# Query normalisation moved behind the rotary products in a two-layer attention and recurrence step

## Chip, cores and metric

The kernel runs on one core of one Trainium2 chip. The metric is device time in microseconds (us); lower is better. TensorE multiplies matrices into PSUM, VectorE (DVE in the profile), ScalarE (ACT) and GpSimd (POOL) do elementwise work, and SyncE (SP) issues most weight transfers. Each engine executes its own queue of instructions in order and waits at semaphores.

## The reference

The reference is one inference step of a two-layer diffusion trunk over 512 latent tokens and 128 context tokens, in float32, with a model width of 1024. Layer 0 is gated attention with 16 query heads and 4 key/value heads of 64; layer 1 is a bidirectional gated linear recurrence. What matters here is how the queries of layer 0 are made:

```python
def _rms_norm(x, g):
    y = xf * lax.rsqrt(jnp.mean(xf * xf, axis=-1, keepdims=True) + NORM_EPS)
    return (y * g.astype(jnp.float32)).astype(x.dtype)

def _attn_project(h, w_in, q_gain, k_gain):
    proj = h @ w_in
    q, k, v, g = jnp.split(proj, ...)
    q = _rms_norm(q.reshape(B, L, N_HEADS, HEAD_DIM), q_gain)
    ...

def _apply_rope(x, cos, sin):      # latent tokens only
    rotated = jnp.concatenate([rot_half(xr), rot_half(xc)], axis=-1)
    return (xf * cos + rotated * sin).astype(x.dtype)
```

Each head of each token is divided by its root mean square, multiplied by a gain, and, for latent tokens, rotated. The factor 1/rms is one number for each token and head, and the rotation is linear in the head's 64 values, so that the factor may stand on either side of the rotation.

## The kernel before

All matrix products of the projections are done as three float32r products of high and low parts (`whi` and `wlo` for weights, `hhi` and `hlo` for activations). Tokens are handled in three units, `UNITS = ((0, 2), (2, 2), (4, 1))`: two pairs of 128-token latent tiles, and one tile of 128 context tokens, called the prompt unit here. The query heads come in four chunks of four heads (256 columns). Chunk 0 is made in `lead_in`, at the start, by functions of its own use (`rms_apply` and `rope_apply` on `q0`), which the change leaves as they are. Chunks 1 to 3 are made by the generator `q_gen`, which runs as a side job of the attention: `weave(att, side, SIDE_B)` advances the side job by 0.62 of a step for each step of the attention, and a `yield` ends a step. Chunk c + 1 may start when the attention's front has reached chunk c.

For each unit `q_gen` does the following. `tok_unit` multiplies 24 or 48 times into one PSUM bank named `qmm`, out of a ring of three banks that the attention's transposes (`pt`), the query transposes (`qps`) and the adaptive projection (`adaps`) share. `rms_stat` squares it on ScalarE (`sq`, L510), sums on VectorE (`ss`, L511), and takes the power -1/2 on GpSimd (`rstd`, L187). After a yield the previous unit's split query is transposed by TensorE (`qps`, L582) and copied to `X` (L584); then a piece of the adaptive projection is made (`fill`, with the loads of its weights), and two more yields follow. Then `rms_apply` multiplies PSUM by `rstd` into `qn` (L524, pinned to the program order), and `rope_apply` makes `u = qn * sin` (L537), `r = qn * cos` (L539) and adds the exchanged halves (L541); for the prompt unit it makes `r = qn * gain` alone (L533). The gain of the latent tokens is folded into the tables `cosq` and `sinq`. After another yield `q_split` writes the high part of `r` with ScalarE (`qs`, L574) and the low part with VectorE (`qs`, L575). The next chunk's `Weights` are split by `split_piece`: `whi` on ScalarE (L221), `wlo` on VectorE (L222), from 512 KB pieces `raw` that the SP queue loads (L208) into a ring of three buffers. The same ring takes the pieces of the adaptive projection, `in_ada_s`.

The attention itself works on score tiles `sc` (L731, L732), takes the negative maximum `nm` on VectorE (L825), the exponential `p` on ScalarE (L828), its scaling by GpSimd (L833), transposes `pt` (L840), and the product with the values `pot` (L758).

The order in which each engine gets its instructions is not simply that of the program: the whole first layer stands in one block, `tc.block(schedule_with_timeline_sim=True)`, whose planner orders instructions by modelled times. An instruction in `tc.keep_in_program_order(...)` is pinned against others so marked.

## Time and profile before

| | |
|---|---|
| median of 3 runs | 873.47 us (872.31 to 873.93) |
| profiled execution, its own time | 873.58 us |
| span of the profiled execution | 871.8 us |
| mean granted TensorE clock | 0.986 |
| TensorE busy | 819.8 us (94%) |
| VectorE busy | 533.8 us (61%) |
| ScalarE busy | 373.0 us (43%) |
| GpSimd busy | 212.9 us (24%) |

The span is the time from the first to the last instruction of the profiled execution. In the tables below an instruction is named by engine, line, operation and tiles, written as output<-input; times are in us from the start of the span. In the views of waits the columns are the total waiting time in us, how often, and the longest. In the views of stretches the columns are the stretch, its length, the busy us and instruction counts of TensorE's matmuls, its weight loads, VectorE, ScalarE and GpSimd, then the granted TensorE clock, the share of DMA engines busy and GB/s. A busy time of TensorE at a granted clock of 0.50 is work that takes about half of that at full clock.

### The profile page before, as it was taken

The numbers are of one execution on the slowest core, as the hardware profiler recorded it, in microseconds if no ns is written. First come the engines' busy times: TensorE is split into PE (matmuls) and PEld (weight loads), VectorE is DVE, ScalarE is ACT, GpSimd is POOL, SyncE is SP. The second block draws the span as 40 slices with busy tenths as digits, with TensorE's granted clock in tenths as the row PEclk, the third lists the DMA queues.
The fourth block names the chain that finished last, engine by engine and source line by source line (L and its number), as shares of the span: only waits on it lengthen the run. The fifth ranks groups of instructions, "written<-read, shape, count | busy, mean of one in ns | idle before, by whom it ended". The sixth has DMA issues, their size and how long they took to land.

```text
span 871.8 us, 19257 instructions
## 1 busy us (share of the span) xinstructions
PE 819.8 (94%) x8120; PEld 732.0 (84%) x8120; DVE 533.8 (61%) x952; ACT 373.0 (43%) x735; POOL 212.9 (24%) x263
## 2 busy tenths in 40 slices
PE   6999999979899988999999999999999999979794
PEld 4789998858778766888899999999999999977683
DVE  3656435735746666676437575758577576757485
ACT  2232536544655767222434444345354443453100
POOL 0213002533424644110001314042333243211010
PEclk9999999989999999999999999999999999989998
DMA  9932212162232253631223323332323232241131
GB/s 339 356 98 85 79 44 74 50 211 87 73 128 67 79 172 120 217 121 40 94 71 72 104 60 88 77 105 68 110 59 114 67 94 84 81 182 50 55 121 48
DMA packets 33991, 92.50 MB, mean 106 GB/s; under 512 B 5025, under 2 KB 12209, under 8 KB 33905
## 3 DMA queue, kind: packets, MB, share of 16 engines
q1 hardware_dynamic: 22416, 71.90, 24.5%
q0 software_dynamic: 4864, 14.44, 5.5%
q10 hardware_dynamic: 6624, 4.93, 1.9%
q8 instruction: 64, 1.05, 0.5%
q14 instruction: 23, 0.18, 0.1%
HBM read 82.06 MB, written 9.19 MB: 105 GB/s over the span
## 4 chain that ended last, share of the span: by engine, by line
PE 85%; DVE 5%; DMA 3%; ACT 3%; issue 1%; POOL 1%; SPq 0%; DVEq 0%; ACTq 0%; POOLq 0%
PE rps L1116 7%; PE rps L1117 6%; PE rps L1118 6%; PE vgps L1106 5%; PE vgps L1108 4%; PE vgps L1107 4%; PE outp L1001 4%; PE outp L1002 4%; PE outp L1003 4%; PE pot L758 3%; PE pt L840 3%; PE lv L1246 2%; PE gps L327 2%; PE gps L328 2%; PE gps L329 2%; PE sc L731 2%
## 5 line engine op out<-in xcount | busy, mean ns | idle before, releaser
L1116 PE MATMUL rps<-h1hi,rhi 128*128 128x320 f32 x368 | 117.9, 320 | 0.0
L1117 PE MATMUL rps<-h1lo,rhi 128*128 128x320 f32 x368 | 113.7, 309 | 0.0
L1118 PE MATMUL rps<-h1hi,rlo 128*128 128x320 f32 x368 | 113.5, 309 | 0.0
L833 POOL TENSOR_SCALAR p<-p,rc 128x640 f32<-128x640 f32 x64 | 54.6, 858 | 70.7 <-DVE rc L832 61.3
L1116 PEld LDWEIGHTS rps<-h1hi,rhi 128*128 128x128 f32 x368 | 69.1, 188 | 1.3
L1117 PEld LDWEIGHTS rps<-h1lo,rhi 128*128 128x128 f32 x368 | 69.2, 188 | 0.0
L1118 PEld LDWEIGHTS rps<-h1hi,rlo 128*128 128x128 f32 x368 | 69.1, 188 | 0.0
L222 DVE TENSOR_TENSOR rlo<-raw,rhi 128x1024 fp32r<-128x1024 f32 x32 | 45.0, 1410 | 33.9 <-ACT rhi L221 33.9
L1274 POOL COPY At<-near 32x160 f32<-32x160 f32 x32 | 14.0, 438 | 201.3 <-DVE near L1236 200.3
L828 ACT ACTIVATE p<-sc,nm 128x640 f32<-128x640 f32 x64 | 51.0, 798 | 24.8 <-DVE nm L825 21.0
L825 DVE TENSOR_REDUCE nm<-sc 128x1 f32<-128x640 f32 x64 | 51.8, 818 | 15.5 <-PE sc L732 15.2
L1224 ACT COPY kc<-A 128x640 f32<-128x640 f32 x40 | 32.2, 804 | 57.7 <-DVE A L1255 51.1
L221 ACT CAST rhi<-raw 128x1024 fp32r<-128x1024 f32 x32 | 33.6, 1049 | 49.9 <-PE rps L1117 47.0
L1106 PE MATMUL vgps<-rhi,h1hi 128*128 128x256 f32 x180 | 51.5, 286 | 1.2 <-ACT h1hi L956 1.2
L840 PE MATMUL pt<-small,p 128*128 128x128 f32 x320 | 50.2, 280 | 2.2 <-DVE acc L316 1.4
L1108 PE MATMUL vgps<-rhi,h1lo 128*128 128x256 f32 x180 | 50.8, 282 | 0.4 <-DVE h1lo L957 0.4
L1107 PE MATMUL vgps<-rlo,h1hi 128*128 128x256 f32 x180 | 50.6, 281 | 0.0
L736 ACT COPY pts<-pt 128x512 f32<-128x512 f32 x64 | 36.2, 589 | 32.9 <-PE pt L840 32.5
L731 PE MATMUL sc<-kk,X 128*128 128x320 f32 x128 | 42.5, 341 | 4.7 <-ACT p L828 4.2
L840 PEld LDWEIGHTS pt<-small,p 128*128 128x128 f32 x320 | 37.1, 142 | 11.2 <-issue 6.2
L1106 PE MATMUL vgps<-wspare,h1hi 128*128 128x256 f32 x140 | 41.6, 297 | 0.0
L327 PE MATMUL gps<-hhi,whi 128*128 128x320 f32 x128 | 40.0, 312 | 0.4 <-ACT X L584 0.4
(265 smaller groups left out, 2373.2 us busy)
## 6 DMA issues: line engine op xcount, KB each, us to landing
raw<-in_rec_w_in SPq DMA_DIRECT2D x40, 512.0 KB, 3.8
raw<-in_ada_s SPq DMA_DIRECT2D x32, 512.0 KB, 3.8
raw<-in_ada_m SPq DMA_DIRECT2D x16, 512.0 KB, 7.7
raw<-in_attn_w_in SPq DMA_DIRECT2D x16, 512.0 KB, 4.3
raw<-in_attn_w_out SPq DMA_DIRECT2D x8, 512.0 KB, 4.2
raw<-in_rec_w_out SPq DMA_DIRECT2D x8, 512.0 KB, 3.5
x1d<-y SPq DMA_DIRECT2D x5, 512.0 KB, 2.6
rx<-x1d POOLq DMA_DIRECT2D x20, 128.0 KB, 3.7
```

The lines of the kernel that those rows point to most:

```text
L327: nc.tensor.matmul(ps[:, :320], w.hi(k)[:, c], hhi[:, k, t], start=(k == 0), stop=False)
L731: nc.tensor.matmul(out, X[:, h, t0:t0 + P], kk[:, c, k0:k1], start=True, stop=False)
L825: nc.vector.tensor_reduce(nm[:, 0:1], sc[:, :, :320], AX.XY, ALU.max, negate=True)
L828: nc.scalar.activation(halves(p[:]), sc[:, :, :320], AF.Exp, bias=nm[:, 0:1], accum_out=su[:, 0:1])
L833: nc.gpsimd.tensor_scalar(p, p, rs[:, 0:1], 1.0, ALU.mult, ALU.mult)
L840: nc.tensor.transpose(pt[:, i * 256 + q * P:i * 256 + (q + 1) * P], ps[q][:, (k0 + i) * P:(k0 + i + 1) * P], ident)
L1106: nc.tensor.matmul(out, h1hi[:, k, t], hi, start=(k == 0), stop=False)
L1107: nc.tensor.matmul(out, h1hi[:, k, t], lo, start=False, stop=False)
L1108: nc.tensor.matmul(out, h1lo[:, k, t], hi, start=False, stop=(k == KT - 1))
L1116: nc.tensor.matmul(ps[:, j, :320], hi[:, k, :], h1hi[:, k, t], start=(k == 0), stop=False)
L1117: nc.tensor.matmul(ps[:, j, :320], hi[:, k, :], h1lo[:, k, t], start=False, stop=False)
L1118: nc.tensor.matmul(ps[:, j, :320], lo[:, k, :], h1hi[:, k, t], start=False, stop=(k == KT - 1))
```

## The change

For chunks 1 to 3 the rotary products read the unnormalised query straight from PSUM, right after `rms_stat`, in a new function `rope_raw`. The multiplication by 1/rms follows three yields later in `rms_scale`, on the result in SBUF. The first instruction of `rope_raw` is pinned to the program order, where `qn` was before; `rms_scale` is not pinned. The prompt unit's gain multiplication moves in the same way. Each latent unit has four VectorE instructions for this as before, each prompt unit two. The title under which the change was made also speaks of "the modulation by four chunks at once"; the diff contains nothing of that kind.

```diff
+    def rope_raw(ps, tt0, n, cos, sin, g):
+
+        w = n * CW
+        r = prep.tile([P, 2 * CW], F32, tag="r", name="r")
+        if tt0 == TS:
+            tc.keep_in_program_order(
+                nc.vector.tensor_tensor(view(r, 0, [[HD, 4 * n], [1, HD]]), ps[:, :w].rearrange("p (h d) -> p h d", d=HD),
+                                        view(g, 0, [[0, 4 * n], [1, HD]]), ALU.mult))
+            return r
+        u = prep.tile([P, 2 * CW], F32, tag="u", name="u")
+        tc.keep_in_program_order(
+            nc.vector.tensor_tensor(heads4(u[:, :w], n), heads4(ps[:, :w], n),
+                                    view(sin, tt0 * HD, [[HD, n], [0, 4], [1, HD]]), ALU.mult))
+        nc.vector.tensor_tensor(heads4(r[:, :w], n), heads4(ps[:, :w], n),
+                                view(cos, tt0 * HD, [[HD, n], [0, 4], [1, HD]]), ALU.mult)
+        nc.vector.tensor_tensor(view(r, 0, [[32, 8 * n], [16, 2], [1, 16]]),
+                                view(r, 0, [[32, 8 * n], [16, 2], [1, 16]]),
+                                view(u, 16, [[32, 8 * n], [-16, 2], [1, 16]]), ALU.add)
+        return r
+
+    def rms_scale(r, n, rstd):
+        qn = prep.tile([P, 2 * CW], F32, tag="qn", name="qn")
+        nc.vector.tensor_tensor(view(qn, 0, [[HD, 4 * n], [1, HD]]), view(r, 0, [[HD, 4 * n], [1, HD]]),
+                                view(rstd, 0, [[1, 4 * n], [0, HD]]), ALU.mult)
+        return qn
 ...
             rstd = rms_stat(ps, n)
+            r = rope_raw(ps, tt0, n, cosq, sinq, qg)
             yield
 ...
-            qn = rms_apply(ps, n, rstd)
-            r = rope_apply(qn, tt0, n, cosq, sinq, qg)
+            qn = rms_scale(r, n, rstd)
             yield
-            pend = (q_split(r, tt0, n, c % 2, X, bank1), n)
+            pend = (q_split(qn, tt0, n, c % 2, X, bank1), n)
```

## The prediction

> **What bounds the kernel now.** I read the page first, for the engine that the time follows.

> ```profile
> span 871.8 us, 19257 instructions
> ...
> PE 819.8 (94%) x8120; PEld 732.0 (84%) x8120; DVE 533.8 (61%) x952; ACT 373.0 (43%) x735; POOL 212.9 (24%) x263
> ...
> PE 85%; DVE 5%; DMA 3%; ACT 3%; issue 1%; POOL 1%; SPq 0%; DVEq 0%; ACTq 0%; POOLq 0%
> ```

> TensorE is busy for 94% of the span and carries 85% of the chain that ended last. The edited code runs on VectorE, at 61%. So the edit moves the time only where TensorE stands still for a query chunk. The attention stage, where chunks 1 to 3 are made, lies at about 140 to 350 us. I asked for busy time there, for two stretches that the later views pointed to, and for whom TensorE waits.

> ```profile
> 140.00:350.00 210.00, 193.60 (x1623) 154.97 (x1622) 127.08 (x284) 124.59 (x271) 87.22 (x96) 0.98 0.32 110
> 184.99:189.19 4.20, 0.00 (x1) 0.03 (x1) 2.74 (x5) 1.45 (x2) 2.12 (x4) 0.93 0.78 264
> 188.63:195.46 6.83, 6.27 (x38) 4.70 (x39) 0.83 (x2) 1.76 (x3) 1.65 (x3) 0.50 0.72 251
> ```

> ```profile
> PE qps L582 <- DVE qs L575: 4.2, 1, 4.2
> PE sc L731 <- ACT p L828: 4.2, 6, 1.7
> PE adaps L265 <- DMA raw<-in_ada_s: 2.0, 2, 1.6
> PE pt L840 <- DVE acc L316: 1.4, 2, 1.1
> ```

> In 210 us TensorE is idle for 210.00 - 193.60 = 16.4 us. The largest single piece is one wait of 4.2 us, for `qs`, the split query of the prompt unit of chunk 1 (184.99 to 189.19). Behind it stand 6.83 us at a granted clock of 0.50; at full clock their 6.27 us of matmuls would take about 3.1. That one wait thus costs about 4.2 + 3.1 = 7.3 us. The chain shows what made it.

> ```profile
> 181.82 3.67 DMA raw<-in_attn_w_in
> 185.49 0.02 issue
> 185.51 1.05 ACT whi L221
> 186.56 0.02 issue
> 186.59 1.22 DVE wlo L222
> 187.81 0.35 DVE r L533
> 188.16 0.02 issue
> 188.18 0.41 ACT qs L574
> 188.59 0.03 issue
> 188.62 0.43 DVE qs L575
> 189.05 0.14 issue
> 189.19 0.72 PE qps L582 x4
> 189.91 0.87 PE pt L840 x4
> 190.78 1.86 PE adaps L265 x16
> ```

> ```profile
> 185.06 0.42 DVE L316 TENSOR_TENSOR acc<-acc,adaps 128x256 f32<-128x256 f32 x1 [2.73 <-PE adaps L265]
> 185.40 0.42 DVE L524 TENSOR_TENSOR qn<-qmm,rstd 128x256 f32<-128x256 f32 x1
> ```

> `qn` was ready at 185.82. The gain multiplication `r`, its follower, stood in VectorE's queue behind `wlo`, the low part of the next chunk's weights; `wlo` waited for `whi`, and `whi` for a weight transfer. So a short step of this unit waited for a transfer of the next.

> **The change part by part.** First the work itself, from the instructions that touch `qn` and from those that touch `u` (durations are minimum/median/maximum in ns).

> ```profile
> L524 DVE TENSOR_TENSOR qn<-qmm,rstd x9: 405/673/681, 156.3 to 294.5; 128x512 f32<-128x512 f32 x6, 128x256 f32<-128x256 f32 x3
> L537 DVE TENSOR_TENSOR u<-qn,sinq x8: 681/692/882, 82.3 to 280.2; 128x512 f32<-128x512 f32 x8
> L539 DVE TENSOR_TENSOR r<-qn,cosq x8: 677/684/686, 82.9 to 281.0; 128x512 f32<-128x512 f32 x8
> L533 DVE TENSOR_TENSOR r<-qn,qg x4: 419/498/889, 95.9 to 295.0; 128x256 f32<-128x256 f32 x4
> ```
> ```profile
> L541 DVE TENSOR_TENSOR r<-r,u x8: 680/691/870, 83.6 to 282.3; 128x512 f32<-128x512 f32 x8
> ```

> A latent unit has four such instructions before and four after; a prompt unit two and two. Before: 673 + 692 + 684 + 691 = 2740 ns. After: the two products read PSUM as L524 does (673 each), the addition is the same (691), and the multiplication by 1/rms reads SBUF twice, as L537 (692) and L539 (684) do; I take 688, between them. That is 2725 ns, 15 less, over six units -0.1 us. The bounds come from the slowest row, 882 ns: if every new multiplication were that slow, +1.1 us; if every old L537 had been, 6 x (882 - 692), another -1.1. For the prompt units I take the same two durations again. VectorE has 210 - 127 = 83 us idle in the stage, so nothing of this lies on the path: zero, and these fractions if that cover were gone.

> [...]

> Next the order. The three rotary instructions move ahead of 1/rms and of three yields, in which the previous unit's transposes, a piece of the adaptive projection with its loads, and attention steps are issued. They wait for TensorE's matmuls alone. They can therefore queue ahead of `ss` and of the softmax maxima `nm`; that is a rival below. The matmuls' PSUM bank is then free without waiting for GpSimd's power; TensorE's waits quoted above name `qn` nowhere as the one that released a bank, so I price that at zero, with a bound of the 1.4 us of its `pt` row on the gaining side. The pinned instruction in the code is now the first product, not `qn`, so loads issued later in program order no longer stand behind an instruction that waits for 1/rms; again zero, as the weight transfer above was issued at 181.82, ahead of `qn` at 185.40.

> What is left behind 1/rms is one VectorE instruction in place of four (two in prompt units). For eight units nobody on TensorE waited on `qs`, so the shorter tail is hidden there. For the ninth I follow the queue. The new `qn` takes the old `qn`'s place, 185.40 to 185.82, and `r` is long done. Two orders are possible.

> Order A: on ScalarE the cast `qs` stands behind `whi`. It runs 186.58 to 186.99; VectorE's half of `qs` stands behind `wlo` (186.59 + 1.22 = 187.81) and ends 0.43 + 0.03 later, at 188.27; with 0.14 of issue TensorE restarts at 188.41 and has been idle for 3.42 us, 0.78 less. The clock fell at 188.63, later than that, so I take it as kept: 3.1 us of work from 188.41 ends at 191.5, where the trace has 195.46. That is -3.9 us; if the clock falls all the same, -0.8.

> Order B: the cast comes ahead of `whi`. It runs 185.84 to 186.25, `qs` ends at 186.71, TensorE restarts at 186.85. Then the next wait is late: `adaps` needs two more weight pieces, of which this is the second.

> ```profile
> 185.05 0.37 SPq L208 DMA_DIRECT2D raw<-in_ada_s  x1
> ```
> ```profile
> raw<-in_ada_s SPq DMA_DIRECT2D x1, 512.0 KB, 4.1
> ```

> It lands at 189.2. At full clock `adaps` takes half of 1.86, and its second half 0.5, so it ends at 189.7. Of the 6.27 us at half clock, 0.72 + 0.87 + 1.86 = 3.45 are `qps`, `pt` and `adaps`; the rest, 2.82, takes 1.4 at full clock. The same point comes at 191.1: -4.4 us. A and B are close, because the transfers hold what the order frees; I take A's -3.9.

> [...]

> Last, the end of chunk 3, where 1/rms came late from GpSimd.

> ```profile
> 294.52 0.43 DVE L524 TENSOR_TENSOR qn<-qmm,rstd 128x256 f32<-128x256 f32 x1 [0.67 <-POOL rstd L187]
> 294.98 0.57 DVE L533 TENSOR_TENSOR r<-qn,qg 128x256 f32<-128x256 f32 x1
> ```
> ```profile
> 298.40 0.87 PE L840 MATMUL pt<-small,p 128*128 128x128 f32 x6 [1.09 <-DVE acc L316]
> ```

> Behind `qn` and `r` VectorE runs without a gap up to `acc`, for which TensorE waits 1.09 us. One instruction fewer brings that forward by 294.98 - 294.52 = 0.46 us: -0.5, and 0 if `acc` is late for another reason.

> The sum is -3.9 - 0.5 = -4.4 us. The profiled execution took 873.58 us for a span of 871.8, so 1.8 us lie around the span; it stands 0.1 above the median of 873.47. From that median I forecast 869.1 us.

> **The rivals.** *Nothing moves.* The new `qn` is no longer pinned and needs 1/rms, as the old `r` needed `qn`; the planner that writes each engine's order may put it where `r` stood, behind `wlo`, at 187.8. Then `qs` comes when it came, and only the 0.5 us at the end of chunk 3 is won: 873.0. For it speaks that `r` was put there once; against it, that `qn`, with the same input from 1/rms, was put ahead.

> *Slower: VectorE is blocked at the products.* Two of them and the addition now come at the end of a unit's matmuls, ahead of `ss` and near an `nm`.

> ```profile
> DVE nm L825 <- PE sc L732: 9.3, 13, 2.1
> ```

> VectorE mostly waits for the scores, so `nm` usually has room. But TensorE's 4.2 us of waits for `p` show places without room, since `p` follows `nm`. Where the products come first, `nm` is late by up to 2 x 673 = 1.35 us in each of six units. All six on the path make +8.1 us; I take half, +4.1, which is 877.6. It decides where the scores' lead over `nm` is shorter than 1.35 us in more than one or two units.

> *Slower: the stretch at half clock comes elsewhere.* The whole block's order is planned from modelled times, so other steps shift too. If another of the three chunk ends meets its weight transfer as chunk 1 did, and the old wait stays, +7.3 us: 880.8.

> **How the numbers follow.** The forecast, in either order, has 0.47; nothing moves 0.13; blocked products 0.28; a second stretch at half clock 0.12. I keep the slower ones this high because the planner sets the order anew, and the profile shows only the old one. A difference of 0.2%, 1.7 us, is about what a measurement of this kernel can tell. That gives faster 0.47, same 0.13, slower 0.40. The forecast's own range is 868.0 (order B, the 0.5, and part of the bank's 1.4) to 872.2 (order A with the clock lost, and the 0.5). The range over all cases goes from 866.0 (order B, the 0.5 and the full 1.4 make 867.2, and the new order may also take most of the longest wait of `sc` for `p`, 1.7) to 879.0, which takes in blocked products with up to two thirds of their bound and leaves out most of the last rival.

> **What would show it.** Right: TensorE's wait for `qs` falls under 3.5 us, no stretch at clock 0.50 stands before 350 us, `r` of the prompt unit runs before `wlo`, and `wlo` no longer stands between `qn`'s input and `qs`. Wrong: `qn` behind `wlo` (nothing moves); more than 4.2 us of waits of `sc` for `p` (blocked products); a new idle time of over 3.5 us before another `qps` or `qmm`. The durations are wrong if the products from PSUM take over 0.70 us.

## The result and the profile after

The changed kernel took 871.77 us (median of 13 runs, 867.86 to 873.53) beside 874.41 us (median of 13 runs) for the kernel before: a ratio of 0.996, with a 95% interval of 0.9941 to 0.9978. That is 2.6 us less by the medians and about 3.5 us by the ratio. Measured once more on another occasion it gave 0.9974 (0.9961 to 0.9986). A second copy of the kernel before, timed against the kernel before, gave 1.0012 (0.9998 to 1.0026), so what differs by about 0.15% isn't told apart here.

The page of the changed kernel's profiled execution (867.86 us, the shortest of its runs) has these lines.

```profile
span 866.1 us, 19260 instructions
...
PE 818.3 (94%) x8120; PEld 730.3 (84%) x8120; DVE 534.0 (62%) x952; ACT 373.0 (43%) x735; POOL 211.8 (24%) x263
...
PE 87%; DVE 4%; ACT 3%; DMA 3%; issue 1%; POOL 0%; SPq 0%; DVEq 0%; ACTq 0%; POOLq 0%
```

The work is what it was: 8120 matmuls, 952 instructions on VectorE and 534 us of its time. The 5.7 us between the two spans are not all the change: the first matmul of chunk 1 starts at 139.2 us, where it was 140.7, although nothing ahead of it was edited. From there to the first matmul of the output projection the two profiles need 208.2 (before) and 204.6 us. I use this stretch, "the stage", below. The next view is whom TensorE waits for in it, in the changed kernel.

```profile
PE sc L757 <- ACT p L854: 2.7, 5, 0.8
PE qps L608 <- DVE qs L601: 2.0, 1, 2.0
PE pt L866 <- ACT pts L762: 1.3, 1, 1.3
PE pot L784 <- DVE pts L762: 1.3, 3, 0.6
PE adaps L265 <- DMA raw<-in_ada_s: 1.2, 1, 1.2
```

The wait for `qs` went from 4.2 to 2.0 us, and the waits of `sc` for `p` from 4.2 us (longest 1.7) to 2.7 (longest 0.8). The chain at the end of chunk 1 now reads:

```profile
179.64 3.43 DMA raw<-in_attn_w_in
183.07 0.02 issue
183.09 1.05 ACT whi L221
184.14 0.02 issue
184.17 1.23 DVE wlo L222
185.39 0.35 DVE qs L601
185.74 0.14 issue
185.88 0.53 PE qps L608 x4
```

The gain multiplication `r` and the cast of `qs` are gone from it: `qs` follows `wlo` at once. From the landing of the weights to TensorE's restart it is 185.88 - 183.07 = 2.81 us; it was 189.19 - 185.49 = 3.70. The weights also landed 0.77 us before TensorE stopped at 183.84 us, where they had landed 0.50 us after it stopped. Three stretches of the changed kernel, the wait, the half clock that followed it, and the 3.41 us ahead of the half clock:

```profile
183.84:185.88 2.04, 0.01 (x2) 0.04 (x1) 1.71 (x3) 0.60 (x2) 0.00 (x0) 1.00 0.66 211
186.21:189.62 3.41, 3.41 (x22) 2.27 (x21) 0.00 (x0) 1.40 (x3) 2.12 (x4) 0.50 0.90 323
182.80:186.21 3.41, 1.38 (x22) 0.75 (x21) 1.89 (x3) 1.35 (x2) 0.50 (x1) 1.00 0.49 166
```

The clock was halved behind the shorter wait too, for 3.41 us in place of 6.83.

### The profile page after: what moved, and what is told of

Same layout as the page of the kernel before. It is cut to its first block, busy times and chain, and to the rows that moved or that the text cites. A ratio compares the mean times of both kernels' runs of the same rounds, so it can differ in the third digit from the quotient of the medians.

```text
span 866.1 us, 19260 instructions
## 1 busy us (share of the span) xinstructions
PE 818.3 (94%) x8120; PEld 730.3 (84%) x8120; DVE 534.0 (62%) x952; ACT 373.0 (43%) x735; POOL 211.8 (24%) x263
## 3 DMA queue, kind: packets, MB, share of 16 engines
q8 instruction: 64, 1.05, 0.5%
## 4 chain that ended last, share of the span: by engine, by line
PE 87%; DVE 4%; ACT 3%; DMA 3%; issue 1%; POOL 0%; SPq 0%; DVEq 0%; ACTq 0%; POOLq 0%
PE rps L1142 7%; PE rps L1143 6%; PE rps L1144 6%; PE vgps L1132 5%; PE vgps L1134 4%; PE vgps L1133 4%; PE outp L1027 4%; PE outp L1028 4%; PE outp L1029 4%; PE pot L784 4%; PE pt L866 3%; PE lv L1272 2%; PE gps L327 2%; PE gps L328 2%; PE gps L329 2%; PE sc L757 2%
## 5 line engine op out<-in xcount | busy, mean ns | idle before, releaser
L859 POOL TENSOR_SCALAR p<-p,rc 128x640 f32<-128x640 f32 x64 | 54.6, 856 | 69.2 <-DVE rc L858 53.1
L222 DVE TENSOR_TENSOR rlo<-raw,rhi 128x1024 fp32r<-128x1024 f32 x32 | 46.0, 1441 | 33.9 <-ACT rhi L221 33.9
L221 ACT CAST rhi<-raw 128x1024 fp32r<-128x1024 f32 x32 | 33.5, 1048 | 51.1 <-PE rps L1143 48.1
L762 ACT COPY pts<-pt 128x512 f32<-128x512 f32 x64 | 36.3, 589 | 29.4 <-PE pt L866 29.2
L784 PE MATMUL pot<-pts,vv 128*64 128x256 f32 x320 | 39.1, 385 | 1.3 <-DVE pts L762 1.3
## 6 DMA issues: line engine op xcount, KB each, us to landing
raw<-in_rec_w_in SPq DMA_DIRECT2D x40, 512.0 KB, 3.6
raw<-in_ada_s SPq DMA_DIRECT2D x32, 512.0 KB, 3.6
raw<-in_ada_m SPq DMA_DIRECT2D x16, 512.0 KB, 8.5
raw<-in_attn_w_in SPq DMA_DIRECT2D x16, 512.0 KB, 4.2
raw<-in_attn_w_out SPq DMA_DIRECT2D x8, 512.0 KB, 4.3
raw<-in_rec_w_out SPq DMA_DIRECT2D x8, 512.0 KB, 3.6
x1d<-y SPq DMA_DIRECT2D x5, 512.0 KB, 2.6
```

The costliest lines, as they stand in the source:

```text
L784: nc.tensor.matmul(pot[j * HD:(j + 1) * HD, :CW], vv[:, slot, c * HD:(c + 1) * HD], moving[j], start=first, stop=last)
L859: nc.gpsimd.tensor_scalar(p, p, rs[:, 0:1], 1.0, ALU.mult, ALU.mult)
```

## The experiments

Three theories stood against each other. T1, the prediction's: the gain comes from the prompt unit of chunk 1, where `r` leaves VectorE's queue behind `wlo`. T2: it comes from the latent units, whose rotary products run early. T3: the planner's old order was unlucky, and any new one would do. All runs are in one table. It has the median of 6 to 13 runs in us and the ratio, with its interval, to runs of the kernel before on the same occasion; their medians lay between 873.5 and 874.8 us, so medians of different rows compare less well than ratios. From each run's one trace it has the time from chunk 1's first `qmm` matmul to chunk 2's, the stage, TensorE's longest wait (or waits) at the end of chunk 1, whatever it waits for, the time at half clock behind it, its longest wait towards the end of chunk 2 (229 to 238 us), and its wait for the transposes `pt` towards the end of chunk 3 (293 to 299 us). A dash means none over 0.5 us.

| kernel | us | ratio | chunk 1 | stage | wait 1 | half clock | wait 2 | wait 3 |
|---|---|---|---|---|---|---|---|---|
| before | 874.41 | | 54.0 | 208.2 | 4.20 | 6.83 | 1.69 | 1.09 |
| the change | 871.77 | 0.9960 (0.9941 to 0.9978) | 51.7 | 204.6 | 2.03 | 3.41 | 0.59 | - |
| the change again | 872.58 | 0.9974 (0.9961 to 0.9986) | 52.4 | 207.4 | 2.30 | 3.41 | 0.59 | - |
| prompt units alone | 871.67 | 0.9958 (0.9941 to 0.9975) | 50.4 | 207.1 | 1.33 | 3.41 | 1.59 | 1.38 |
| latent units alone | 870.46 | 0.9945 (0.9926 to 0.9965) | 54.8 | 205.6 | 3.98 | 6.83 | 0.77 | - |
| unpinned | 868.07 | 0.9929 (0.9911 to 0.9947) | 51.8 | 202.1 | 2.24 | 3.41 | - | - |
| placebo `acc` | 875.16 | 1.0016 (1.0000 to 1.0031) | 54.1 | 209.8 | 4.25 | 6.83 | 1.59 | 1.13 |
| placebo `ss` | 874.70 | 1.0017 (1.0002 to 1.0032) | 54.7 | 208.3 | 1.62 + 1.62 + 2.31 | 6.83 | 1.60 | 1.12 |
| bank held | 872.06 | 0.9981 (0.9966 to 0.9996) | 53.8 | 205.3 | 4.66 | 6.83 | 0.77 | - |
| unpinned, `qs` first | 868.56 | 0.9950 (0.9935 to 0.9965) | 49.7 | 204.2 | 2.42 | 3.41 | 0.54 | - |
| before again | 875.38 | 1.0012 (0.9998 to 1.0026) | 54.4 | 210.2 | 4.56 | 6.83 | 1.59 | 1.12 |
| before, kept busy | 874.29 | 1.0007 (0.9991 to 1.0022) | 52.2 | 208.9 | 0.97 + 0.85 | - | 2.08 | 1.12 |
| unpinned again | 869.53 | 0.9944 (0.9920 to 0.9969) | 53.1 | 204.4 | 2.22 | 6.83 | - | - |
| unpinned, kept busy | 866.11 | 0.9907 (0.9887 to 0.9927) | 51.4 | 200.8 | 0.58 | - | - | - |

**The change again.** No edit.

> The whole change once more, for a second profile. Both theories: 0.994 to 0.998 of the time before. Chunk 1 (first qmm of chunk 1 to first qmm of chunk 2) takes 51 to 52.5 us where the profile before has 54.0; TensorE waits 1.5 to 3.4 us for qs of chunk 1's prompt unit; the first 139 us, which the change does not touch, may differ by 1 to 2 us from profile to profile.

Wait and chunk 1 came as expected. The stage took 2.8 us longer than in the first profile of the same program. Most of it lies behind 300 us: a wait for a piece of the adaptive projection was 1.71 us in place of 1.25, and a window at half clock followed it (318.5 to 321.9 us), which the first profile doesn't have. A single profile's stage is thus good to about 3 us, and the ratios decide.

**The two halves of the change.**

```diff
-            r = rope_raw(ps, tt0, n, cosq, sinq, qg)
+            r = rope_raw(ps, tt0, n, cosq, sinq, qg) if tt0 == TS else None   # prompt units alone; latent alone: tt0 != TS
...
-            qn = rms_scale(r, n, rstd)
+            if r is not None:
+                qn = rms_scale(r, n, rstd)
+            else:
+                qn = rope_apply(rms_apply(ps, n, rstd), tt0, n, cosq, sinq, qg)
```

> Only the prompt units (128 context tokens) take the new form; the latent units normalise first, as before. Theory T1 (the gain comes from the prompt unit of chunk 1: its gain multiplication r no longer stands in VectorE's queue between wlo and qs): the whole gain, 0.994 to 0.997; the planned order even puts qs ahead of the second wlo, so TensorE's wait for qs falls to 2 us or less and chunk 1 takes 51.5 us or less. Theory T2 (the gain comes from the latent units: the rotary products that run before 1/rms, the PSUM bank that is free earlier, and the order that the planner makes of it): 0.998 to 1.002, chunk 1 at 53 to 55 us.

> Only the latent units take the new form; the prompt units normalise first, as before, and their planned order is wlo, acc, qn, r, qs, all behind the second wlo. T1: no gain, 0.998 to 1.003; TensorE's wait for qs stays at 3.5 to 5 us, and the stretch at clock 0.50 behind it stays. T2: the gain, 0.994 to 0.997.

The prompt units alone gave 0.9958, as T1 had it. VectorE's order of time at the end of chunk 1 in that kernel:

```profile
182.71 0.42 DVE L550 TENSOR_TENSOR qn<-r,rstd 128x256 f32<-128x256 f32 x1 [0.81 <-POOL rstd L187]
183.61 0.42 DVE L601 TENSOR_TENSOR qs<-qn,qs 128x256 fp32r<-128x256 f32 x1 [0.47 <-ACT qs L600]
184.21 0.42 DVE L316 TENSOR_TENSOR acc<-acc,adaps 128x256 f32<-128x256 f32 x1 [0.18 <-PE adaps L265]
185.91 1.22 DVE L222 TENSOR_TENSOR wlo<-raw,whi 128x1024 fp32r<-128x1024 f32 x1 [1.28 <-ACT whi L221]
```

`qs` starts 2.3 us ahead of `wlo`, TensorE doesn't wait for it at all, and chunk 1 takes 50.4 us. The 1.33 us that the table has there are a wait of the prompt's scores for `X`, the copy of the transposed queries. This is order B of the prediction.

But the latent units alone gave 0.9945, where T1 expected no gain, although the first two lines of TensorE's waits show the old wait standing:

```profile
PE qps L608 <- DVE qs L601: 4.0, 1, 4.0
PE sc L760 <- ACT p L857: 2.5, 4, 1.2
```

So T1's mechanism is there, and T1's claim to the whole gain falls. Two later waits tell the halves apart, and they sort all kernels of the table: those with the old latent form (before twice, prompt units alone, both placebos, before kept busy) wait 1.59 to 2.08 us at the end of chunk 2 and 1.09 to 1.38 us at the end of chunk 3; the eight with the new latent form wait at most 0.77 us at the one and under 0.5 us at the other. The first gain is clear in TensorE's whole idle time in chunk 2, 2.9 to 3.4 us in the six and 0.5 to 2.1 us in the eight. The second is partly made up by other waits, of scores `sc` for `p` among them: from chunk 3's first matmul to the output projection the idle time is 7.9 to 9.4 us in the six and 6.7 to 8.2 us in the eight. At the end of chunk 2 of the kernel before, VectorE's order of time is:

```profile
231.68 1.23 DVE L222 TENSOR_TENSOR wlo<-raw,whi 128x1024 fp32r<-128x1024 f32 x1 [1.32 <-ACT whi L221]
232.82 1.54 DVE L825 TENSOR_REDUCE nm<-sc 128x1 f32<-128x640 f32 x2
```
```profile
234.70 0.41 PE L731 MATMUL sc<-kk,X 128*128 128x320 f32 x1 [1.69 <-ACT p L828]
```

Two maxima `nm` stand behind a `wlo` that waits for weights. That load was issued at 225.96 us, 31.3 us after chunk 2's first matmul; in the changed kernel at 220.29, after 29.4, and with the latent units alone after 28.1, since the piece of the adaptive projection that frees its buffer is earlier in TensorE's order (it ends 239 and 233 matmuls behind the chunk's first, where it was 257). There `wlo` is over before the scores are needed. At the end of chunk 3 GpSimd's order differs; its order of time before, and with the change:

```profile
287.39 4.56 POOL L957 TENSOR_TENSOR hlo<-gs,hhi 128x640 fp32r<-128x640 f32 x3
291.94 1.56 POOL L833 TENSOR_SCALAR p<-p,rc 128x640 f32<-128x640 f32 x2
293.47 1.01 POOL L187 TENSOR_TENSOR rstd<-rs_t,mhalf 128x4 f32<-128x4 f32 x1
```
```profile
279.18 4.62 POOL L983 TENSOR_TENSOR hlo<-gs,hhi 128x640 fp32r<-128x640 f32 x3 [1.83 <-PE qmm L336]
283.77 0.80 POOL L859 TENSOR_SCALAR p<-p,rc 128x640 f32<-128x640 f32 x1
284.54 1.55 POOL L983 TENSOR_TENSOR hlo<-gs,hhi 128x640 fp32r<-128x640 f32 x1
286.06 0.80 POOL L859 TENSOR_SCALAR p<-p,rc 128x640 f32<-128x640 f32 x1
286.83 1.02 POOL L187 TENSOR_TENSOR rstd<-rs_t,mhalf 128x4 f32<-128x4 f32 x1
```

Three subtractions `hlo` of a later step (4.6 us) stood just ahead of `rstd`; now they run 7.6 us ahead of it. This order alone is not shown to be the cause: in the run with `qs` first, GpSimd still has four `hlo` (6.1 us) and two `p` straight ahead of `rstd`, and TensorE's wait for `pt` is 0.4 us. That these waits go with the latent form is shown by the sorting; through which dependence the planner comes to its new order is not.

**The pin left out.** The first product is not pinned.

```diff
-        tc.keep_in_program_order(
-            nc.vector.tensor_tensor(heads4(u[:, :w], n), ...))
+        nc.vector.tensor_tensor(heads4(u[:, :w], n), ...)      # and the same for the prompt unit's product
```

> The whole change, but the first product of each unit is not pinned to the program order, so the planner lays out everything anew while the prompt unit of chunk 1 keeps the order qn, wlo, qs of the changed kernel. T1: the gain stays, 0.994 to 0.998, with a wait for qs of 1.5 to 3.4 us. T2 (the order of the latent units is what counts): the gain is lost or changes by more than 0.2%, that is outside 0.994 to 0.998.

> The unpinned form of the change once more, on the same chip as the others of this call: 0.991 to 0.995.

0.9929 and 0.9944: the gain doesn't hang on the pin, and the second figure held what was expected of it. The first lies outside T1's range, as T2 allowed; in that profile TensorE has no wait of over 0.3 us between 187 and 281 us.

**Two placebos.** No step is changed; one instruction of the kernel before is pinned, so that the planner gives a new order.

```diff
-                nc.vector.tensor_tensor(acc, acc, ps[:, :CW], ALU.add)
+                tc.keep_in_program_order(nc.vector.tensor_tensor(acc, acc, ps[:, :CW], ALU.add))    # placebo acc
-        nc.vector.tensor_reduce(ss, ...)
+        tc.keep_in_program_order(nc.vector.tensor_reduce(ss, ...))                                  # placebo ss, q_gen's units alone
```

> The kernel before with no step changed; only the accumulation acc of the adaptive projection is pinned to the program order, so the planner lays out some stretches anew, while the end of chunk 1 keeps its order (qn, wlo, r, qs). T1 (the wait for qs at the end of chunk 1 is what the change shortens) and T2 (the early rotary products of the latent units bring a gain of their own): 0.998 to 1.002, with a wait for qs of about 4 us. T3 (the planner's order of before is an unlucky one, and any other order is as good as the change): 0.993 to 0.998.

> The kernel before with no step changed; the sum of squares ss of each unit is pinned to the program order. At the end of chunk 1 the planned order becomes wlo, acc, qn, r, qs, the same as with only the latent units changed. T1: 0.999 to 1.004, with a wait for qs of 3.5 to 5 us. T2: the same, as the latent units have the old form; the 0.9945 of the run with the latent units changed is then due to their form. T3: 0.993 to 0.998.

1.0016 and 1.0017, little more than the 1.0012 of the copy of the kernel before and inside its interval. T3 falls for these two orders. With `ss` pinned the wait at the end of chunk 1 fell into three, of 5.55 us together, and only 2.31 us of it were for `qs`, where 3.5 to 5 were expected.

**The bank held.**

```diff
             qn = rms_scale(r, n, rstd)
+            held = tiny.tile([P, 1], F32, tag="held", name="held")
+            tc.keep_in_program_order(nc.vector.tensor_tensor(held, ps[:, 0:1], rstd[:, 0:1], ALU.mult))
```

> The whole change, but a one-element product that reads the unit's PSUM bank (its result is used nowhere) stands right behind the multiplication by 1/rms, so the bank is held as long as before; nine instructions of about 0.15 us are added on VectorE. T1: the gain stays, 0.994 to 0.999, as r is still out of the tail. T2 in the form that the early release of the bank is the gain: 0.998 to 1.003. T3: 0.993 to 0.999.

0.9981 lies inside T1's range and, by 0.0001, inside that of T2's bank form, so the time doesn't tell them apart. The waits at the ends of chunks 2 and 3 stay away (0.77 us and none), so an early release of the bank is not what removed them. What was lost is chunk 1, where the wait is 4.66 us again. With the new pin the order changed as well, so the loss there can't be put down to the bank.

**`qs` first.** `whi` and `wlo` of the weights of chunks 2 and 3 and `qs` of the prompt units are pinned.

```diff
+        hold = tc.keep_in_program_order if src[0] == "attn_w_in" and 2 <= src[1] <= 3 else (lambda ins: ins)
-        nc.scalar.copy(hi, raw)
+        hold(nc.scalar.copy(hi, raw))       # the same for lo, and for both halves of qs where tt0 == TS
```

> The change without the pin on the first product, and with the split qs of the prompt units and the split of the next chunk's weights (whi, wlo) pinned, so that qs stands ahead of whi on ScalarE and of wlo on VectorE. T1: no wait of over 0.6 us for qs at the end of chunk 1 and no stretch at clock 0.50 there, and 2 to 3 us less than the unpinned kernel: 0.987 to 0.992 of the time before. If another wait (the weight pieces of the adaptive projection) takes its place, or T2 or T3 holds: 0.991 to 0.995, as the unpinned kernel.

0.995: the expectation of T1 missed, and the other one, that another wait takes the place, held at its edge. TensorE doesn't wait for `qs` any more, and this came instead, with half clock behind it (188.9 to 192.3 us):

```profile
187.49 0.64 PE L266 MATMUL adaps<-raw,sil 128*32 128x256 f32 x8 [2.42 <-DMA raw<-in_ada_s]
```

For this piece of the weights TensorE waits 2.42 us; the prediction had named it as what is late next.

**The control, and TensorE kept busy.** Where `qs` is late, 20 transposes whose result is used nowhere run ahead of the waiting ones.

```diff
             pend = (q_split(r, tt0, n, c % 2, X, bank1), n)
+            if tt0 == TS and c == 1:
+                warm = bank1("warm")
+                for i in range(20):
+                    nc.tensor.transpose(warm[:, i % 4 * P:(i % 4 + 1) * P], qn[:, i % 2 * P:(i % 2 + 1) * P], ident)
```

> The kernel before once more, as a control and for a second profile. All theories: 0.9985 to 1.0015; TensorE's wait for qs at the end of chunk 1 is 4.0 to 4.4 us, the waits of about 1.6 us (sc for p, end of chunk 2) and 1.1 us (pt, end of chunk 3) are there again.

> The kernel before, with 20 transposes of chunk 1's prompt qn whose result is used nowhere, put on TensorE ahead of the query transposes that wait for qs; at 0.11 us each they fill about 2.2 us of the wait of 4.2 us and leave the wait's end where it is. If the clock falls after a window of 3.4 us in which TensorE was busy for less than about half, and this costs what the prediction put on it: no stretch at clock 0.50 behind the wait, and 2 to 3 us less, 0.9965 to 0.998. If the lost clock is worth nothing, since the pieces of the adaptive projection's weights come no sooner: 0.999 to 1.001.

> The unpinned form with the 20 idle transposes ahead of the waiting query transposes of chunk 1. Its wait for qs was 2.2 us, with one window of 3.4 us at clock 0.50 behind it; the transposes can start when qn is there, fill part of the wait and may push its end by up to 1 us. If the clock is kept: 0.5 to 1.5 us less than without them, 0.990 to 0.994; if the push takes it back, the same as without them, 0.991 to 0.996.

The control gave 1.0012, inside its range, and the two later waits came again; the wait for `qs` was 4.56 us, a little over the 4.0 to 4.4 expected. In the kernel before the block does what it should to the clock. The wait's end stays at 189.04 us, and nothing behind it runs at half clock:

```profile
185.81 2.37 PE L618 MATMUL warm<-small,qn 128*128 128x128 f32 x20 [0.97 <-DVE qn L524]
189.04 0.51 PE L582 MATMUL qps<-identr,qs 128*128 128x128 f32 x4 [0.85 <-DVE qs L575]
```

Chunk 1 takes 52.2 us beside 54.0 and 54.4, so the lost clock was worth 1.8 to 2.1 us there. But the ratio, 1.0007, is that of the control within the intervals. The expected gain was missed; the time fits the second case, that the lost clock is worth nothing because the weights come no sooner. Two rows of TensorE's waits show where at least part of it went:

```profile
PE sc L735 <- ACT p L832: 4.5, 6, 2.1
PE adaps L265 <- DMA raw<-in_ada_s: 2.4, 2, 2.0
```

TensorE comes sooner to the later waits for weights and stands longer: the longest wait of `sc` is 2.1 us (1.7 and 1.6 in the two profiles of before), that of `adaps` 2.0 (1.6 and 1.2), and behind each the clock is halved for 3.41 us. In the unpinned kernel, which has no wait at the end of chunks 2 and 3, the same block goes with 0.9907 where the kernel without it has 0.9944 on the same chip; the two intervals meet (0.9920 to 0.9927), so this extra 0.4% is likely and not shown. By the medians it is 3.4 us, more than the 0.5 to 1.5 expected. It is the fastest kernel of the study, 7.6 us under the median of the kernel before on the same occasion (873.67 us).

## Why the prediction was right, and where not

The forecast, 869.1 us, 4.4 us less, was right in direction, in range, and in its first reason. That it came so near the measured gain is partly luck: two errors of opposite sign, below, nearly cancel. Its steps one by one:

*VectorE's work unchanged:* right. The products from PSUM took 685 and 682 ns (medians), where the prediction took 673 and put its limit at 0.70 us. The new multiplication by 1/rms had a median of 677 ns, with a longest of 1101, where 688 was taken.

*Order A at the end of chunk 1:* right to the step; `qn`, `wlo`, `qs` on VectorE and `whi`, `qs` on ScalarE. The saving from landing to restart was 0.89 us, where 0.78 was worked out. The wait shrank by more, 2.2 us, as the weights landed 1.27 us earlier relative to TensorE's stop. Of the prediction's signs of being right, the wait under 3.5 us and the early `r` came; that `wlo` no longer stands between `qn` and `qs` did not, and order A, on which the sum rests, never had it so.

*The clock kept, -3.1 us:* wrong. It fell behind a wait of 2.03 us, and in the prompt-only kernel behind one of 1.33. One window in place of two was saved. With the shorter wait chunk 1 gained 2.3 and 1.6 us in the two profiles, where 3.9 was forecast; order B, in the prompt-only kernel, gained 3.6 where 4.4 was forecast. The step took the clock as kept because TensorE would restart 0.22 us before the fall. But with a restart at 188.41 us TensorE would have been busy for 0.22 us of the 3.41 us that end at 188.63, and the runs show a fall behind every such window with TensorE busy for under 1.5 us. Why one window was saved is also in the records. In the kernel before, the clock fell at 188.63, and the wait went on to 189.19; the first window at half clock had TensorE busy for 2.85 us and was followed by a second. In the changed kernel TensorE restarted at 185.88, ahead of the fall at 186.21, was busy for the whole of the first window, and had full clock behind it. The section on the hardware below has the counts.

*The end of chunk 3, -0.5 us:* the wait of 1.09 us went away whole, but not for the reason given. In the prompt-only kernel, which has one instruction fewer behind 1/rms just as well, it is 1.38 us. It goes with the latent form.

*Nothing from the eight other units:* wrong, and the largest error. The step looked only for waits of TensorE on `qs`, and priced the new order at zero. The latent form alone gave 0.9945, 4.3 us by the medians; the two later waits, about 2 us shorter together, are part of it, and the rest is not traced. This error and that on the clock nearly cancel in the sum.

*The rivals.* `qn` did not fall behind `wlo`. The products did not block VectorE: TensorE's waits for `p` fell from 4.2 to 2.7 us. No second stretch at half clock came at another chunk's end; the window at 318.5 us in the second profile of the change stands behind a late piece of the adaptive projection.

The halves don't add up: 0.9958 and 0.9945 would make 0.990, and the whole has 0.996 and 0.9974. In the whole change the planner took order A at the end of chunk 1, in the prompt units alone order B, which is 1.4 to 2.0 us of it. Another part shows in TensorE's records of the stage. The whole change has less idle time, 12.2 and 13.4 us in its two profiles where the two of before have 16.4 and 16.8, but the same 1608 matmuls are busy for longer: 190.7 and 190.6 us, with time at half clock counted half, beside 188.6 and 188.7 before. The prompt units alone have 189.9, the latent units alone 188.8, and both profiles of the unpinned form 188.4. So about 2 us of the idle time won came back as longer matmuls, and without the pin they did not. What makes them longer, or whether short waits are counted as work there, is not shown.

## What to carry to other kernels

Where a planner writes the order from modelled times, a change that leaves the work as it is (533.8 and 534.0 us on VectorE here) can still move the time (0.996), through what happens to stand in an in-order queue behind an instruction that waits for a late transfer (here `r` and `qs` behind `wlo`, a wait of TensorE's of 4.20 us); look for short steps queued behind an instruction that waits for a load, on every engine of the chain. A placebo, an edit that changes the order alone, helps to tell a form's own gain from luck. Where TensorE waits for transfers that are issued by its own progress, time won ahead of them may be given back at the next one (with TensorE kept busy the longest wait for a piece of `in_ada_s` was 2.0 us, where the two profiles of before have 1.6 and 1.2).

## What the runs showed of the hardware

```profile
184.19:187.60 3.41, 2.08 (x18) 1.84 (x19) 1.68 (x3) 2.02 (x3) 2.12 (x4) 1.00 0.80 305
187.60:191.01 3.41, 3.41 (x20) 2.27 (x20) 1.92 (x4) 1.94 (x9) 0.74 (x1) 0.51 0.67 183
```

and in the kernel before, around the wait of 1.69 us, no fall came behind a window with 1.72 us busy:

```profile
233.01:236.42 3.41, 1.72 (x13) 1.71 (x14) 3.41 (x9) 2.06 (x5) 0.56 (x1) 1.00 0.46 154
236.42:239.83 3.41, 3.41 (x32) 2.28 (x31) 2.33 (x5) 3.05 (x6) 2.00 (x3) 1.00 0.00 0
```

Counted over all fourteen profiles, behind the first 20 us: every window at full clock with TensorE busy for under 1.5 us was followed by half clock, none with over 2.1 us was, and between these both happened. The way back was narrower: every window at half clock with TensorE busy for 2.93 us or less was followed by another one, every one with 2.95 us or more by full clock. The busy times rest on modelled ends of the matmuls. So the wait of 1.33 us in the prompt-only kernel cost a window, by an estimate 1.7 us of work (half of 3.41), and the one of 4.20 us in the kernel before, which ran on into the half clock by 0.56 us (188.63 to 189.19), a second. In the first profile of the unpinned kernel a wait of 2.24 us cost one window; in the second, 2.22 us and a wait of 0.59 us across the window's edge cost two. This may be part of why executions of one program differ here by 0.6% (871.62 to 876.82 us for the kernel before on the last occasion), which is not shown.

VectorE and GpSimd: some VectorE instructions grew when they began while GpSimd was at work. Between 140 and 350 us the fourteen profiles hold 372 of `u`, `r`, `qn` and `qs` that read two SBUF operands, and 101 of these grew by over 0.06 us. All 101 began while GpSimd was scaling a `p` or subtracting an `hlo`, and they ended after it by nearly the same time, 0.53 to 0.55 us where they are 512 wide and 0.27 to 0.29 us where they are 256 wide, as if they had stood still until GpSimd was done. Not every one that began so grew. The 174 others, which read PSUM, took at most 0.01 us more than usual, 67 of them with GpSimd at work when they began. In the changed kernel the new `qn` is of the first kind: 677 ns (median), but 1101 ns from 169.98 us, beside a `p` from 169.46 to 170.54. The small `rs_t`, elsewhere 0.16 us, took 1.43 once there. Its end, 286.10 us, is that of the `hlo` of 284.54 us in the rows of GpSimd's above.

```profile
284.67 1.43 DVE L186 TENSOR_SCALAR rs_t<-ss 128x4 f32<-128x4 f32 x1
```
